# One more seven-product pair at the head of a feed-forward block: chunks 0 and 1 of the up-projection, and block sums of x from float copies

## The chip, the cores and the metric

The kernel runs on one core of a Trainium2 chip. A time is the device time of one execution in microseconds (us). TensorE (PE in the profile) does the matrix products, VectorE (DVE) and ScalarE (ACT) the elementwise work, GpSimd (POOL) a few elementwise operations and DMA issues, SyncE (SP) most DMA issues. Each engine takes its instructions strictly in the order in which they were written; a wait on a semaphore holds everything behind it on that engine.

## The reference

Two decoder layers over a residual stream h of 512 tokens by 1024 features, in float32. Each layer has an attention part (dilated windows in the first, forgetting attention with shared keys and values in the second), and then the part that matters here, the same in both layers:

```
def conv_ffn(xn, w_up, cw, cb, w_down):
    a = xn @ w_up                                  # (512, 1024) @ (1024, 5632)
    ap = jnp.pad(a, ((0, 0), (CONV_W - 1, 0), (0, 0)))
    a = sum(ap[:, j:j + T] * cw[j] for j in range(CONV_W)) + cb
    gate, val = jnp.split(a, 2, axis=-1)
    return (jax.nn.gelu(gate, approximate=True) * val) @ w_down
...
    h = h + rms_norm(mix, g[1])
    f = conv_ffn(rms_norm(h, g[2]), w_up[l], conv_w[l], conv_b[l], w_down[l])
    h = h + rms_norm(f, g[3])
```

## The kernel before

**Numbers.** Every operand of a product is split into a high part (rounded to the format that TensorE takes, by ScalarE) and a low part (the rest, by VectorE), and each product is three matmuls: high times high, high times low, low times high (`mm3`). The low part of some weights is made in another way: ScalarE writes the high part and the negated weight, and a DMA issued by GpSimd adds the weight and the parts up (`high_added`, or `high(key, True)`).

**The hidden features** are 22 chunks of 128, each with a gate and a value half, so two output tiles of 128 features by 512 tokens a chunk, one PSUM bank each. A chunk computed directly is two products over the whole of x (`up`, 24 matmuls of 512 columns each, or `feat_mm` in two halves of 256 columns). After it come the convolution (`tap`: one ScalarE and two VectorE operations a tile), the GELU and the product of gate and value (`product`), which goes to a DRAM buffer by a GpSimd DMA.

**Pairs.** Chunks 4 to 19 are taken two at a time as a 2 by 2 block product with seven instead of eight multiplications (class `Pair`). The weight blocks are called A11, A21, A22, A12 and their sums S1 to S4; x is cut into four blocks (features by tokens), and XA and XB hold sums of those blocks. The seven products are p_1 to p_7, each 24 matmuls of 256 columns. Several of them share a PSUM bank, and between them ScalarE copies a finished half aside (`keep_1`, `keep_7`, `keep_2`; the tile csum), to be added in later by VectorE (`sum_1`, `sum_3`, `sum_4`). The loop over the pairs interleaves seven products of one pair with the weight preparation of the next and the taps of the one before.

**The boundary ahead of it.** The attention's output projection ends in four blocks of 128 tokens. For each block, ScalarE and VectorE normalise it and add it into h, then normalise h (a square with a sum, a square root and a reciprocal, then `xn`), TensorE transposes it (eight transposes into the tiles xt_ps), ScalarE casts the high part and VectorE subtracts for the low part (`transpose_in`). Blocks 0 and 1 are through before the up-projection begins. Blocks 2 and 3 are transposed between the first products, which so far need only the first 256 tokens (LO): that is `first_products`, chunks 0 and 1, four tiles by LO, then four by HI.

**x block sums** (`sums_in`, tile xsum): GpSimd adds the high and low parts of x back together, VectorE makes the block differences, and ScalarE and VectorE split these into XA and XB. Chunks 2 and 3 run directly behind chunks 0 and 1, which covers this work; then the pairs begin.

**Order.** All of it is written out by hand (`manual_schedule`): the order of the program is the order on each engine. Weights are loaded by SP's queue through ten buffers (`W.load`), in the order of the list `pieces`, and prepared `W.ahead` pieces before they are used.

Of the kernel before, what the change touches and what calls it, by code (L numbers as in the profile page):

```python
# [9 lines left out]
F32 = mybir.dt.float32  # L10
# [14 lines left out]
BIG = 3.0e38  # L25


PAIRS = tuple(range(4, 20, 2))
ND = NF // 2
LAST = 3  # L30

# [84 lines left out]
def trunk_kernel(ctx, tc, x, norm_gains, w_qkv_a, w_o_a, w_q_b, w_o_b, kv_norm, w_kvf, b_f,  # L116
# [63 lines left out]
    dT = [tc.dram_tile([ND, 128, 2048], F32, name=f"dT{l}") for l in range(2)]  # L180

    def add_ffn(l):
        for c in range(NF):
            if c in PAIRS:
                for q, f in ((0, 0), (0, DFF), (1, DFF), (1, 0)):
                    add_block(w_up[l], q, f + c * 128)
            elif c - 1 not in PAIRS:
                add_cols(w_up[l], c * 128)
                add_cols(w_up[l], DFF + c * 128)
# [160 lines left out]
        lo = [t8([128, 4, T], F32R, name=f"{name}l{i}") for i in range(2)]  # L350
        return hi, lo

    def transpose_in(b, xn, xT, between=None):

        pts = []
        for i in range(2):
            pt = bank([128, 4, 128], name="xt_ps")
            for k in range(4):
                pe.transpose(pt[:, k, :], xn[:, (4 * i + k) * 128:(4 * i + k + 1) * 128], ident)
            pts.append(pt)  # L360
        s = slice(b * 128, b * 128 + 128)
        for i, pt in enumerate(pts):
            if i and between is not None:
                between()
            hi, lo = xT[0][i], xT[1][i]
            act.copy(hi[:, :, s], pt)
            dve.tensor_tensor(lo[:, :, s], pt, hi[:, :, s].bitcast(F32), ALU.subtract)

    def xs(xT, kc, s):
        return xT[0][kc // 4][:, kc % 4, s], xT[1][kc // 4][:, kc % 4, s]  # L370
# [60 lines left out]
    class Boundary:  # L431
# [26 lines left out]
        def transpose(self, b):  # L458
            if self.xT is None:
                self.xT = new_xT(self.name)  # L460
            transpose_in(b, self.xn.pop(b), self.xT)

    class SharedBoundary(Boundary):

# [76 lines left out]
                self.out(b)  # L541


    def first_products(bd, n):
        bd.norm(3)
        outs = [bank([128, T], name="first") for _ in range(n)]
        ws = []
        for i, o in enumerate(outs):
            ws.append(W.get())
            feat_mm(ws[i], bd.xT, o, LO)  # L550
            if i == 0:
                bd.transpose(2)
            if i == 2:
                bd.transpose(3)
        for w, o in zip(ws, outs):
            feat_mm(w, bd.xT, o, HI)
        return outs


    def load_conv(l):  # L560
        rows = t2([44, 4, 128], name="cv_rows")
        for j in range(3):
# [53 lines left out]
    def ffn(l, bd, cp, nxt, gain, ahead):  # L616
# [4 lines left out]
        def tap(bb, c, s, ps):  # L621
# [2 lines left out]
            dve.scalar_tensor_tensor(bb[:, s, 1:], ps[:, :T - 1], cp[:, 1, ch:ch + 1], bb[:, s, 1:], ALU.mult, ALU.add)  # L624
            dve.scalar_tensor_tensor(bb[:, s, 2:], ps[:, :T - 2], cp[:, 0, ch:ch + 1], bb[:, s, 2:], ALU.mult, ALU.add)

        class Chunk:

            def __init__(self, c, banks, room=None):
# [14 lines left out]

            def product(self):
                c = self.c
                if c - 1 in hc:
                    pool.dma_start(hD[c - 1], hc.pop(c - 1))
# [6 lines left out]

        def sums_in():

            v = [t8([128, 4, T], name=f"xsum{i}") for i in range(2)]
            for i in range(2):
                pool.tensor_tensor(v[i], xT[0][i].bitcast(F32), xT[1][i].bitcast(F32), ALU.add)  # L660
            yield
            dve.tensor_tensor(v[0][:, :, LO], v[0][:, :, HI], v[0][:, :, LO], ALU.subtract)
            dve.tensor_tensor(v[0][:, :, HI], v[1][:, :, HI], v[0][:, :, HI], ALU.subtract)
            yield
            dve.tensor_tensor(v[1][:, :, HI], v[1][:, :, HI], v[0][:, :, LO], ALU.subtract)
            dve.tensor_tensor(v[1][:, :, LO], v[1][:, :, LO], v[1][:, :, HI], ALU.subtract)
            yield
            for X, src in ((XA, v[0]), (XB, v[1])):
                X += [t8([128, 4, T], F32R, name="xsh"), t8([128, 4, T], F32R, name="xsl")]
                for k in (0, 2):  # L670
                    act.copy(X[0][:, k:k + 2], src[:, k:k + 2])
                    dve.tensor_tensor(X[1][:, k:k + 2], src[:, k:k + 2], X[0][:, k:k + 2].bitcast(F32), ALU.subtract)
                    yield

        def X(i):
            return xT[0][i], xT[1][i]
# [1 line left out]
        class Pair:  # L678
# [33 lines left out]
                dve.tensor_tensor(w[:, 1], self.f[key], w[:, 0].bitcast(F32), ALU.subtract)  # L712

            def prod(self, key, outs, x, s, start=False):
                w = self.t.pop(key).rearrange("p s (k c) -> p s k c", k=4)
                for i, o in enumerate(outs):
                    half_mm(o, w[:, :, :, i * 128:i * 128 + 128], x, s, start)

            def new_banks(self):
                return [bank([128, T], name="up") for _ in range(2)]  # L720
# [237 lines left out]

        def half_mm(o, w, x, s, start):
            for k in range(4):  # L960
                mm3(o, w[:, 0, k, :], w[:, 1, k, :], x[0][:, k, s], x[1][:, k, s], start and k == 0, k == 3, True)

        def up(w, o, kcs):
            wh, wl = (t.rearrange("p (k c) -> p k c", k=8) for t in w)
# [4 lines left out]
        base = W.n_get  # L969
        first = first_products(bd, 4)  # L970
        xT = bd.xT
        extra = sums_in()
        next(extra)
        done, last = Chunk(0, first[0:2]), Chunk(1, first[2:4])
        done.taps()
        next(extra)
        done.product()
        last.taps()
        W.ahead, W.ahead_dma = 1, 3
        W.split(base + 7)  # L980
        W.high_added()
        pairs = [Pair(c) for c in PAIRS]
        p, n = pairs[0:2]

        banks = p.new_banks()
        up(W.get(), banks[0], range(KD))
        for _ in range(3):
            next(extra, None)
        p.take("A11", "A21", "A22")
        p.high("A11", True)  # L990
        p.s1()
        p.s3()
        up(W.get(), banks[1], range(KD))
        run(extra)
        p.high("S1", True)
        done, last = last, Chunk(2, banks)

        banks = p.new_banks()
        up(W.get(), banks[0], range(KD))
        done.product()  # L1000
        last.tap(0)
        p.high("S3")
        p.s2()
        last.tap(1)
        p.high("S2")
        last.gelu()
        p.take("A12")
        p.low("S3")
        p.s4()
        up(W.get(), banks[1], range(KD))  # L1010
        p.high("A22", True)
        p.low("S2")
        last.product()
        n.take("A11")
        n.high("A11", True)
        p.p_1()
        p.keep_1()
        prev, m = None, [Chunk(3, banks)]

        for i, p in enumerate(pairs):  # L1020
            W.n_get += 4
            n, n2 = (pairs[i + k] if i + k < len(pairs) else None for k in (1, 2))
            a, b = m[0], m[-1]
            p.p_7()
            if prev:
                prev.sum_1()
            a.tap(0)
            p.high("A12", True)
# [12 lines left out]
            if prev:  # L1041
                b.tap(0)
            a.product()
            p.low("S4")
            p.p_5()
            p.sum_3()
            if n:
                n.s3()
            if prev:
                b.tap(1)  # L1050
            if n:
                n.high("A22", True)
# [12 lines left out]
            p.p_2()  # L1065
# [58 lines left out]
        pair_sums(3)  # L1124
        pair_lows(2)
        last.product()
        pool.dma_start(hD[NF - 1], hc.pop(NF - 1))

        down(nxt, ahead)
        W.ahead = 4  # L1130
# [776 lines left out]
```

## Time and profile before

| | |
|---|---|
| time, median of three runs | 1104.31 us (1103.82 to 1104.97) |
| the profiled execution | 1104.32 us, its span 1102.5 us, mean granted TensorE clock 0.998 |
| TensorE matmul busy | 1093.6 us, 99% of the span |
| VectorE, ScalarE, GpSimd busy | 892.3, 735.1, 231.5 us |
| the head of the up-projection in layer 0, first matmul to the first product p_7 | 178.0 to 227.4 us |
| the same head in layer 1 | begins at 759.8 us |

Rows of the profile have the start and the duration in us, the engine, the line in the kernel, the operation, output and input tiles, their sizes, and in brackets how long the engine had been idle and what released it. A duration runs to the end of the write; the next instruction on the same engine starts a little before that, so prices of queues are taken from one start to the next.

### The profile page before, as it was taken

To read this page: it belongs to the slowest core of one execution; us is meant where nothing else is said; L and a number is where in the kernel's file an instruction comes from. 1 tells how busy PE (TensorE), PEld (TensorE's weight loads), DVE (VectorE), ACT (ScalarE), POOL (GpSimd) and SP (SyncE) were. 2 spreads that over 40 slices of the span, in tenths; PEclk is the share of its full clock that TensorE was granted. 3 is DMA by queue.
4 is the path that set the end of the run, shared out by engine and by line. 5 is a ranking of instruction groups with operands and counts; after the bars stand their busy time and mean duration, and the time that the engine had idled before them with its cause. 6 is when DMAs were issued, how large, how long until landed. Compare 5 with 4: busy or idle time off the path is not lost.

```text
span 1102.5 us, 18986 instructions
## 1 busy us (share of the span) xinstructions
PE 1093.6 (99%) x6905; PEld 968.5 (88%) x6905; DVE 892.3 (81%) x1453; ACT 735.1 (67%) x1232; POOL 231.5 (21%) x335
## 2 busy tenths in 40 slices
PE   9999999999999999999999999999999999999997
PEld 6988889899999988888878888889999999988886
DVE  5897788967887789997698677868967887789994
ACT  6754575777788766576562588856677787856572
POOL 2632001322122211000000545600412122211000
PEclk9999999999999999999999999999999999999999
DMA  9699855499999999793447666783499999998872
GB/s 325 184 356 410 317 174 151 91 227 231 224 224 248 230 295 325 277 338 101 134 153 268 210 159 169 216 265 117 98 224 231 231 221 247 224 296 313 317 249 76
DMA packets 156006, 252.06 MB, mean 229 GB/s; under 512 B 12352, under 2 KB 99384, under 8 KB 155912
## 3 DMA queue, kind: packets, MB, share of 16 engines
q1 hardware_dynamic: 137576, 186.61, 51.1%
q0 software_dynamic: 18336, 64.24, 26.3%
q8 instruction: 54, 0.88, 0.3%
q14 instruction: 40, 0.33, 0.1%
HBM read 166.08 MB, written 39.63 MB: 187 GB/s over the span
## 4 chain that ended last, share of the span: by engine, by line
PE 85%; issue 9%; DVE 2%; ACT 2%; DMA 1%; POOL 1%; DVEq 0%; SPq 0%; POOLq 0%; ACTq 0%
PE up L288 12%; PE up L289 12%; PE up L290 12%; PE acc L288 8%; PE acc L290 8%; PE acc L289 8%; PE qk_ps L289 2%; PE qk_ps L288 2%; PE qk_ps L290 2%; PE s_ps L1733 2%; PE o_ps L1781 2%; PE pT_ps L1766 1%; PE first L290 1%; PE first L288 1%; PE first L289 1%
## 5 line engine op out<-in xcount | busy, mean ns | idle before, releaser
L288 PE MATMUL up<-xsh,w 128*128 128x256 f32 x512 | 144.9, 283 | 0.0
L289 PE MATMUL up<-xsl,w 128*128 128x256 f32 x512 | 144.9, 283 | 0.0
L290 PE MATMUL up<-xsh,w 128*128 128x256 f32 x512 | 144.9, 283 | 0.0
L288 PE MATMUL acc<-w 128*128 128x512 f32 (+1 forms) x311 | 120.7, 388 | 0.3 <-DVE mix L337 0.3
L290 PE MATMUL acc<-w 128*128 128x512 f32 (+1 forms) x311 | 120.6, 388 | 0.1
L705 ACT CAST w<-wraw 128x1024 fp32r<-128x1024 f32 x80 | 82.6, 1048 | 37.7 <-DVE wraw L689 37.7
L624 DVE SCALAR_TENSOR_TENSOR bb<-up,conv,bb 128x511 f32<-128x511 f32 x80 | 59.8, 748 | 57.2 <-ACT bb L623 57.0
L289 PE MATMUL acc<-w 128*128 128x512 f32 (+1 forms) x267 | 103.2, 387 | 0.0
L288 PEld LDWEIGHTS up<-xsh,w 128*128 128x128 f32 x512 | 98.3, 192 | 0.0
L289 PEld LDWEIGHTS up<-xsl,w 128*128 128x128 f32 x512 | 98.3, 192 | 0.0
L290 PEld LDWEIGHTS up<-xsh,w 128*128 128x128 f32 x512 | 98.3, 192 | 0.0
L623 ACT ACTIVATE bb<-up,conv 128x512 f32<-128x512 f32 x80 | 60.2, 780 | 32.7 <-DVE up L775 24.3
L288 PE MATMUL up<-xbh,w 128*128 128x256 f32 (+1 forms) x256 | 80.0, 312 | 0.1
L288 PE MATMUL up<-xch,w 128*128 128x256 f32 (+1 forms) x256 | 80.0, 312 | 0.1
L289 PE MATMUL up<-xbl,w 128*128 128x256 f32 (+1 forms) x256 | 79.2, 310 | 0.0
L289 PE MATMUL up<-xcl,w 128*128 128x256 f32 (+1 forms) x256 | 79.2, 310 | 0.0
L290 PE MATMUL up<-xbh,w 128*128 128x256 f32 (+1 forms) x256 | 79.2, 309 | 0.0
L290 PE MATMUL up<-xch,w 128*128 128x256 f32 (+1 forms) x256 | 79.2, 309 | 0.0
L708 POOL DMA_DIRECT2D w<-wraw x48 | 40.4, 841 | 183.5 <-ACT w L707 96.5
L76 DVE TENSOR_TENSOR w<-wraw,w 128x1024 fp32r<-128x1024 f32 x48 | 65.0, 1376 | 11.9 <-ACT w L58 11.4
L58 ACT CAST w<-wraw 128x1024 fp32r<-128x1024 f32 x62 | 63.7, 1051 | 15.8 <-PE v_ps L289 6.9
L290 PEld LDWEIGHTS acc<-w 128*128 128x128 f32 x311 | 58.4, 188 | 12.9 <-DVE w L817 0.9
(308 smaller groups left out, 3279.6 us busy)
## 6 DMA issues: line engine op xcount, KB each, us to landing
wraw<-in_w_up_dram SPq DMA_DIRECT2D x88, 512.0 KB, 6.6
w<-wraw POOLq DMA_DIRECT2D x62, 512.0 KB, 7.6
dT<-dsums SPq DMA_DIRECT2D x28, 512.0 KB, 7.5
dsums<-in_w_down_dram SPq DMA_DIRECT2D x22, 512.0 KB, 7.5
dsums<-in_w_down_dram SPq DMA_DIRECT2D x44, 256.0 KB, 6.6
hD<-hc POOLq DMA_DIRECT2D x44, 256.0 KB, 7.3
wraw<-dT SPq DMA_DIRECT2D x22, 512.0 KB, 6.8
dact<-hD SPq DMA_DIRECT2D x44, 256.0 KB, 5.3
```

Source lines behind the costliest of these rows:

```text
L58: self.nc.scalar.copy(pair[:, 0], raw)
L76: self.nc.vector.tensor_tensor(pair[:, 1], raw, pair[:, 0].bitcast(F32), ALU.subtract)
L288: pe.matmul(o, ah, bh, start=first, stop=False, skip_group_check=shared)
L289: pe.matmul(o, ah, bl, start=False, stop=False, skip_group_check=shared)
L290: pe.matmul(o, al, bh, start=False, stop=last, skip_group_check=shared)
L623: act.activation(bb[:, s, :], ps, AF.Identity, bias=cp[:, 3, ch:ch + 1], scale=cp[:, 2, ch:ch + 1])
L624: dve.scalar_tensor_tensor(bb[:, s, 1:], ps[:, :T - 1], cp[:, 1, ch:ch + 1], bb[:, s, 1:], ALU.mult, ALU.add)
L705: act.copy(w[:, 0], self.f[key])
L708: pool.dma_start(w[:, 1], self.f[key], accum_op=ALU.add)
L1733: pe.matmul(s[hh][:, :nn], qT[j][:, m, hh, i * 128:(i + 1) * 128], k, start=m == 0, stop=m == 1)
L1766: pe.transpose(o[:, k0 + k, :], p[:, hh, k * 128:(k + 1) * 128], ident)
L1781: pe.matmul(o[64 * hh:64 * hh + 64, i * 128:(i + 1) * 128], Vt[hd // 8][:, k, (hd % 8) * 64:(hd % 8) * 64 + 64], pT[j, i, hh][:, k, :], st ...
```

## The change

Chunks 0 and 1 are no longer computed directly but become one more pair, the first in the list `PAIRS`. The head is written anew: the product p_1 of this pair, the transposes of block 2, chunk 2's gate half by LO, the product p_2, the transposes of block 3, chunk 2's value half by LO, then both by HI, then chunk 3 directly, then the loop over the pairs, which for the first pair leaves out p_2 and A12. Since p_1 and p_2 of that pair use A11 and A12 before their sums are formed, these two blocks are loaded and split on their own and A11 and A12 loaded a second time for the sums. GpSimd's two additions go. In their place, ScalarE copies each transposed block once more, unrounded, into the tile xsum (two copies a block), and VectorE's block differences are made in two parts, 128 tokens at a time. The eight copies stand in `transpose_in`, behind the casts.

```
-PAIRS = tuple(range(4, 20, 2))
+PAIRS = 0, *range(4, 20, 2)
...
-    def transpose_in(b, xn, xT, between=None):
+    def transpose_in(b, xn, xT, keep):
...
             act.copy(hi[:, :, s], pt)
             dve.tensor_tensor(lo[:, :, s], pt, hi[:, :, s].bitcast(F32), ALU.subtract)
+        for i, pt in enumerate(pts):
+            act.copy(keep[i][:, :, s], pt)
...
-            v = [t8([128, 4, T], name=f"xsum{i}") for i in range(2)]
+            v = bd.x32
             for i in range(2):
-                pool.tensor_tensor(v[i], xT[0][i].bitcast(F32), xT[1][i].bitcast(F32), ALU.add)
-            yield
...
+                lo, hi = (slice(o + i * 128, o + i * 128 + 128) for o in (0, 256))
+                dve.tensor_tensor(v[0][:, :, lo], v[0][:, :, hi], v[0][:, :, lo], ALU.subtract)
+                dve.tensor_tensor(v[0][:, :, hi], v[1][:, :, hi], v[0][:, :, hi], ALU.subtract)
+                dve.tensor_tensor(v[1][:, :, hi], v[1][:, :, hi], v[0][:, :, lo], ALU.subtract)
+                dve.tensor_tensor(v[1][:, :, lo], v[1][:, :, lo], v[1][:, :, hi], ALU.subtract)
+                yield
...
+        W.ahead, W.ahead_dma = 1, 3
+        bd.norm(3)
+        p.t["A11"], w0, p.t["A12"], w1 = (W.get() for _ in range(4))
+        banks = [bank([128, T], name="first") for _ in range(2)]
+        p.p_1()
+        W.high_added()
+        bd.transpose(2)
+        feat_mm(w0, xT, banks[0], LO)
+        sums = sums_in()
+        next(sums)
+        p.keep_1()
+        W.high_added()
+        p.p_2()
+        bd.transpose(3)
+        feat_mm(w1, xT, banks[1], LO)
+        next(sums)
+        feat_mm(w0, xT, banks[0], HI)
+        feat_mm(w1, xT, banks[1], HI)
+        W.ahead_dma = 1
+        p.take("A11", "A21", "A22")
+        p.s1()
+        p.s3()
+        p.s2()
+        next(sums)
+        done, banks = Chunk(2, banks), p.new_banks()
+        done.tap(0)
+        p.high("S3")
+        p.high("S2")
+        p.take("A12")
+        p.s4()
+        up(W.get(), banks[0], range(KD))
+        next(sums)
+        done.tap(1)
+        done.gelu()
+        p.high("S1", True)
+        p.low("S3")
+        p.low("S2")
+        up(W.get(), banks[1], range(KD))
+        p.high("A22", True)
+        done.product()
+        n.take("A11")
+        n.high("A11", True)
```

ScalarE's order at block 3's norm (the square of h) and block 2's transposes, layer 0, in the kernel before. The number of partitions and elements follows the tiles; in brackets stands whose semaphore the row waits for.

```order
L295 ACTIVATE junk,s_1978<-h 128x1024 [waits DVE_49]
L297 ACTIVATE sd<-s_1978,eps_t 128x1 [waits Activation_49]
L366 CAST xbh_1858<-xt_ps 128x4x128 [waits PE_49]
L366 CAST xbh_1859<-xt_ps 128x4x128 [waits PE_49]
L58 CAST w<-wraw 128x1024 [waits DMAHW6_49]
L58 CAST w<-wraw 128x1024 [waits DMAHW7_49]
```

The same place in the changed kernel, up to the next weight:

```order
L299 ACTIVATE junk,s_1984<-h 128x1024 [waits DVE_49]
L301 ACTIVATE sd<-s_1984,eps_t 128x1 [waits Activation_49]
L58 CAST w<-wraw 128x1024 [waits DMAHW6_49]
L69 ACTIVATE w<-wraw 128x1024
L368 CAST xbh_1858<-xt_ps 128x4x128 [waits PE_49]
L368 CAST xbh_1859<-xt_ps 128x4x128 [waits PE_49]
L371 COPY xsum_1862<-xt_ps 128x4x128 [waits DVE_49]
L371 COPY xsum_1863<-xt_ps 128x4x128 [waits DVE_49]
L719 COPY csum<-up 128x256 x2
L58 CAST w<-wraw 128x1024 [waits DMAHW7_49]
```

A weight's cast and its negation now stand ahead of block 2's casts, the two float copies behind them, each waiting for VectorE, and then the two csum copies of `keep_1`.

TensorE's order in the changed kernel where chunk 2's gate half by LO ends (first) and p_2 begins (up, with the second feature half of x):

```order
L292 MATMUL first<-xbh_1859,w 128x256
L293 MATMUL first<-xbl_1861,w 128x256
L294 MATMUL first<-xbh_1859,w 128x256
L292 MATMUL up<-xbh_1859,w 128x256 [waits Activation_49]
L293 MATMUL up<-xbl_1861,w 128x256
L294 MATMUL up<-xbh_1859,w 128x256
```

Before, there stood at this place the third tile of `first_products` behind the second; now the first matmul of p_2 waits for ScalarE, into the bank from which `keep_1` copies.

More of the change, by code (lines that the diff above doesn't have):

```diff
@@ L182, in add_ffn @@
     def add_ffn(l):
[L183 to L189, printed above, removed]
+        for q in range(2):
+            add_block(w_up[l], q, 0)
+            add_cols(w_up[l], q * DFF + 2 * 128)
+        for q in range(2):
+            add_cols(w_up[l], q * DFF + 3 * 128)
+        for c in PAIRS:
+            for q, f in ((0, 0), (0, DFF), (1, DFF), (1, 0)):
+                add_block(w_up[l], q, f + c * 128)
+        for c in (NF - 2, NF - 1):
+            for q in range(2):
+                add_cols(w_up[l], q * DFF + c * 128)
         for j in range(ND):
@@ L362, in transpose_in @@
         for i, pt in enumerate(pts):
-            if i and between is not None:
-                between()
             hi, lo = xT[0][i], xT[1][i]
@@ L460, in transpose @@
                 self.xT = new_xT(self.name)
-            transpose_in(b, self.xn.pop(b), self.xT)
+                self.x32 = [t8([128, 4, T], name=f"xsum{i}") for i in range(2)]
+            transpose_in(b, self.xn.pop(b), self.xT, self.x32)
     class SharedBoundary(Boundary):
@@ L541, in part @@
                 self.out(b)
[L544 to L557, printed above, removed]
     def load_conv(l):
@@ L625, in tap, with send @@
             dve.scalar_tensor_tensor(bb[:, s, 2:], ps[:, :T - 2], cp[:, 0, ch:ch + 1], bb[:, s, 2:], ALU.mult, ALU.add)
+        def send():
+            for c in list(hc):
+                pool.dma_start(hD[c], hc.pop(c))
         class Chunk:
@@ L646, in product @@
                 c = self.c
-                if c - 1 in hc:
-                    pool.dma_start(hD[c - 1], hc.pop(c - 1))
+                send()
                 hc[c] = t2([128, T], name="hc")
@@ L672, in sums_in @@
                     dve.tensor_tensor(X[1][:, k:k + 2], src[:, k:k + 2], X[0][:, k:k + 2].bitcast(F32), ALU.subtract)
-                    yield
+                yield
         def X(i):
@@ L714, in prod @@
             def prod(self, key, outs, x, s, start=False):
-                w = self.t.pop(key).rearrange("p s (k c) -> p s k c", k=4)
+                w = self.t.pop(key)
+                w = [(w[i] if type(w) is tuple else w[:, i]).rearrange("p (k c) -> p k c", k=4) for i in range(2)]
                 for i, o in enumerate(outs):
-                    half_mm(o, w[:, :, :, i * 128:i * 128 + 128], x, s, start)
+                    half_mm(o, [t[:, :, i * 128:i * 128 + 128] for t in w], x, s, start)
             def new_banks(self):
@@ L960, in half_mm @@
             for k in range(4):
-                mm3(o, w[:, 0, k, :], w[:, 1, k, :], x[0][:, k, s], x[1][:, k, s], start and k == 0, k == 3, True)
+                mm3(o, w[0][:, k, :], w[1][:, k, :], x[0][:, k, s], x[1][:, k, s], start and k == 0, k == 3, True)
         def up(w, o, kcs):
@@ L967, in up @@
                 mm3(o, wh[:, kc, :], wl[:, kc, :], bh, bl, kc == 0, kc == KD - 1)
-        base = W.n_get
-        first = first_products(bd, 4)
         xT = bd.xT
[L972 to L981, printed above, removed]
         pairs = [Pair(c) for c in PAIRS]
         p, n = pairs[0:2]
-        banks = p.new_banks()
@@ L986, in ffn @@
-        up(W.get(), banks[0], range(KD))
-        for _ in range(3):
-            next(extra, None)
+        W.ahead, W.ahead_dma = 1, 3
[11 more added lines that the diff above has]
+        p.p_2()
@@ L989, in ffn @@
+        bd.transpose(3)
[4 more added lines that the diff above has]
+        W.ahead_dma = 1
         p.take("A11", "A21", "A22")
-        p.high("A11", True)
         p.s1()
         p.s3()
-        up(W.get(), banks[1], range(KD))
-        run(extra)
-        p.high("S1", True)
[L996 to L1007, printed above, removed]
+        p.s2()
[10 more added lines that the diff above has]
+        done.gelu()
+        p.high("S1", True)
         p.low("S3")
-        p.s4()
+        p.low("S2")
@@ L1010, in ffn @@
         up(W.get(), banks[1], range(KD))
         p.high("A22", True)
-        p.low("S2")
-        last.product()
+        done.product()
         n.take("A11")
         n.high("A11", True)
-        p.p_1()
-        p.keep_1()
+        W.ahead_dma = 3
         prev, m = None, [Chunk(3, banks)]
@@ L1027, in ffn @@
             a.tap(0)
-            p.high("A12", True)
+            if prev:
+                p.high("A12", True)
             p.keep_7()
@@ L1064, in ffn @@
                 n.high("S1", True)
-            p.p_2()
+            if prev:
+                p.p_2()
             if n:
@@ L1126, in ffn @@
         last.product()
-        pool.dma_start(hD[NF - 1], hc.pop(NF - 1))
+        send()
         down(nxt, ahead)
```

6 lines of the change are left out of this document (removed).

## The prediction

> **What bounds the kernel now.** I read the page's first part, then TensorE's waits, then its order of time at the head of a feed-forward block. In the fence, by line: busy time; who was waited for, total, times, longest; then start, duration, instruction.
>
> ```profile
> PE 1093.6 (99%) x6905; PEld 968.5 (88%) x6905; DVE 892.3 (81%) x1453; ACT 735.1 (67%) x1232; POOL 231.5 (21%) x335
> ...
> PE warm L248 <- DVE zero L243: 1.2, 1, 1.2
> ...
> 174.39 1.03 PE L359 MATMUL xt_ps<-ident,xn 128*128 128x128 f32 x8
> 178.01 0.28 PE L288 MATMUL first<-xbh,w 128*128 128x256 f32 x1
> 180.88 1.04 PE L359 MATMUL xt_ps<-ident,xn 128*128 128x128 f32 x8
> 187.50 1.03 PE L359 MATMUL xt_ps<-ident,xn 128*128 128x128 f32 x8
> 202.76 0.40 PE L288 MATMUL up<-xbh,w 128*128 128x512 f32 x1
> 224.55 0.28 PE L288 MATMUL up<-xbh,w 128*128 128x256 f32 x1
> 227.42 0.28 PE L288 MATMUL up<-xsh,w 128*128 128x256 f32 x1
> 247.58 0.28 PE L288 MATMUL up<-xsh,w 128*128 128x256 f32 x1
> ```
>
> TensorE bounds it: 1093.6 of 1102.5 us, and no wait over 1.2 us, none of them in this head. So each matmul removed counts in full, and so does each wait added. The prices come from starts. From 227.42 (first product of one pair) to 247.58 (the same of the next) lie seven products of 24 matmuls: 20.16 us for 168, 0.120 each at 256 columns. From 202.76 to 224.55 lie 96 matmuls of 512 columns: 0.227 each. Eight transposes take 0.87 (start 180.88, and the 48 matmuls to 187.50 take 5.76).
>
> **Matmuls removed.** Before, chunks 0 and 1 are 192 matmuls at 256 columns (23.04 us), chunks 2 and 3 are 96 at 512 (21.8), together 44.8 us. Now the pair is 168 at 256 (20.16), chunk 2 is 96 at 256 (11.52), chunk 3 is 48 at 512 (10.9), together 42.56. That is 2.24 us less in each layer, 4.5 in all. It stands only if the other engines keep up in the new head.
>
> **What is added to ScalarE's queue.** Each of the four x blocks gets two copies of its transposes to float, and by the order of rows each waits for VectorE, whose low-part subtraction reads the same bank. Behind them stand the squares of the next block's norm; ahead of the csum copies (keep_1, at 190 us below) stand block 2's casts and copies and a weight's cast and negation. The second product p_2 (line 292, "up", second half of x) waits on ScalarE: it writes the bank that keep_1 reads. So I walk ScalarE (ACT) and VectorE (DVE) from block 0 on with the rows of before:
>
> ```profile
> 168.84 1.07 ACT L366 CAST xbh<-xt_ps 128x512 fp32r<-128x512 f32 x2
> 169.78 1.08 ACT L295 ACTIVATE junk<-h 128x1024 bf16<-128x1024 f32 x1
> 176.12 1.08 ACT L295 ACTIVATE junk<-h 128x1024 bf16<-128x1024 f32 x1
> 181.29 1.06 ACT L295 ACTIVATE junk<-h 128x1024 bf16<-128x1024 f32 x1 [2.06 <-DVE h L344]
> 182.68 1.05 ACT L366 CAST xbh<-xt_ps 128x512 fp32r<-128x512 f32 x2
> 205.74 1.06 ACT L69 ACTIVATE w<-wraw 128x1024 fp32r<-128x1024 f32 x1
> L511 ACT COPY nT<-xt_ps 128x512 f32<-128x512 f32 x8 | 4.3, 583 | 0.0
> 226.18 0.37 ACT L728 COPY csum<-up 128x256 f32<-128x256 f32 x1 [2.59 <-PE up L290]
> ...
> 169.69 1.28 DVE L367 TENSOR_TENSOR xbl<-xt_ps,xbh 128x512 fp32r<-128x512 f32 x2
> 171.58 1.41 DVE L309 SCALAR_TENSOR_TENSOR xn<-h,rs,gain 128x512 f32<-128x512 f32 x2
> 172.91 0.68 DVE L337 TENSOR_TENSOR mix<-acc,gain 128x512 f32<-128x512 f32 x1
> 173.70 1.28 DVE L344 SCALAR_TENSOR_TENSOR h<-mix,rs,h 128x1024 f32<-128x1024 f32 x1
> 175.98 1.28 DVE L367 TENSOR_TENSOR xbl<-xt_ps,xbh 128x512 fp32r<-128x512 f32 x2
> 177.85 1.42 DVE L309 SCALAR_TENSOR_TENSOR xn<-h,rs,gain 128x512 f32<-128x512 f32 x2
> 179.97 1.28 DVE L344 SCALAR_TENSOR_TENSOR h<-mix,rs,h 128x1024 f32<-128x1024 f32 x1
> 188.76 1.29 DVE L367 TENSOR_TENSOR xbl<-xt_ps,xbh 128x512 fp32r<-128x512 f32 x2 [0.88 <-ACT xbh L366]
> ```
>
> The copies' price is L511's row, the same form: 0.58 us, the next instruction 0.47 after its start (1.07 for two casts).
>
> - Block 0: its low parts end at 169.69 + 1.28 = 170.97, so the second copy starts at 171.0 and the square of block 1 at 171.5, not 169.78 (+1.7). The normalised rows xn start 1.80 after the square (169.78 to 171.58): 173.3. TensorE transposes them at 174.4, still in time.
> - Block 1: after xn, VectorE needs 1.33 (171.58 to 172.91), 0.79 to the sum into h, 1.20 for that, 0.67 for the next mix: low parts from 177.3 to 178.55, not 177.26. p_1 needs the first half at 178.1: in time. Second copy 178.6, square of block 2 at 179.05, not 176.12 (+2.9). xn 1.73 later: 180.8, its halves done at 181.5 and 182.2. The transposes are due at 180.88 and now end at 182.7 instead of 181.75. **First wait: 0.9 us.**
> - Block 3's norm: h is summed at 180.8 + 2.12 = 182.9, done 184.2; its square starts there instead of 181.29, and frees ScalarE 1.39 later (181.29 to 182.68): 185.6. Then the weight's cast and negation, about 0.95 each: 187.5. Then block 2's casts, which before stood at 182.68. VectorE's low parts start 0.6 later and end 1.28 after that: 189.4. The second copy starts there, the first csum copy 0.47 later at 189.9, done 0.37 later: 190.3.
> - TensorE: transposes to 182.7, chunk 2's first half 2.88: p_2 is due at 185.55 and starts at 190.3. **Second wait: 4.75 us.**
>
> Bounds: with the two earlier copy pairs free, square 3 stays at 181.29 and the csum copy ends at 187.4 for a p_2 due at 184.63: 2.75 us in all. With 0.2 more at each of six handoffs: 6.9. I take the walk, 5.65, since every link has its row. Layer 1 repeats it.
>
> **Clock.** No stretch of before has such a gap inside, but both ends show TensorE's clock. In the window rows PEclk is the third number from the right:
>
> ```profile
> 1096.33 0.28 PE L290 MATMUL acc<-w 128*128 128x256 f32 x1
> 1098.00:1098.50 0.50, 0.00 (x0) 0.00 (x0) 0.50 (x2) 0.00 (x0) 0.00 (x0) 1.00 0.00 0
> 1098.70:1099.00 0.30, 0.00 (x0) 0.00 (x0) 0.30 (x1) 0.00 (x0) 0.00 (x0) 0.50 0.00 0
> 1.22 1.46 PE L248 MATMUL warm<-zero 128*128 128x512 bf16 x3 [1.22 <-DVE zero L243]
> 2.82 0.61 PE L248 MATMUL warm<-zero 128*128 128x512 bf16 x1
> 6.54 0.59 PE L248 MATMUL warm<-zero 128*128 128x512 bf16 x2
> ```
>
> The last matmul ended at 1096.6, and by 1098.7, 2 us later, the clock stood at one half. At the start, three matmuls of 0.61 end to end took 1.46 (0.42 apart); the last two are about 0.2 apart at 6.54: half speed for up to 5.3 us of work, 2.65 lost. So a gap of 4.75 us likely halves the clock, and p_2 and what follows lose 0 to 2.65 per layer. I take 2.0, nearer the upper end, as the fall needed only 2 us.
>
> The Trainium skill ("TensorE: Matmul & The Clock Gate", section "What's actually happening") has the clock fall after an idle window of about 3.4 us and rise after one as long of work. By it the loss would be 1.7 and the total 0.6 lower; a gap at my lower bound (2.75) would cost nothing, where the row of 2 us says it could. The row decides here.
>
> **What stays covered.** The rows that price it; the last two are DMA issues with their size and median time to landing:
>
> ```profile
> 189.53 10.19 POOL L660 TENSOR_TENSOR xsum<-xbh,xbl 128x2048 f32<-128x2048 f32 x2 [52.12 <-DVE xbl L367]
> 207.93 2.35 DVE L672 TENSOR_TENSOR xsl<-xsum,xsh 128x1024 fp32r<-128x1024 f32 x2
> 215.46 0.74 DVE L624 SCALAR_TENSOR_TENSOR bb<-up,conv,bb 128x511 f32<-128x511 f32 x1
> w<-wraw POOLq DMA_DIRECT2D x6, 512.0 KB, 5.6
> wraw<-in_w_up_dram SPq DMA_DIRECT2D x88, 512.0 KB, 6.6
> ```
>
> GpSimd's two additions go, which held only the block sums and nothing on TensorE. The new work behind block 3's transposes must end before the pair's S3 product, which TensorE reaches after 0.87 + 3 x 2.88 + 10.9 = 20.4 us. VectorE starts 1.26 after the transposes' start (187.50 to 188.76): low parts 1.3, four block subtractions 2.6 with 0.5 of waiting for copies, nine 1024-wide operations up to S3's low part at about 1.15 (10.4; L672: 2.35 for two), two taps at 1.45 each (twice 0.74): 17.7 in all, so done at 19.0 of 20.6 (S3's low part is read 0.24 after the first matmul). The margin of 1.6 us makes it free; beyond it each us counts. A22's low part comes by GpSimd's accumulating DMA (5.6 us to landing), about 24 after the transposes, and is read at 26.4. The second load of A11 and the reordered ones stand in SP's queue at least 10 us ahead of their readers, against 6.6 to landing.
>
> **Sum.** Per layer -2.24 + 0.9 + 4.75 + 2.0 = +5.4; twice, +10.8. The profiled execution took 1104.32 us (span 1102.5), the median of the runs shown is 1104.31, so the forecast is 1115.1.
>
> **Rivals.**
> - Forecast, stall with the clock halved: 1115.1, chance 0.58.
> - The same stall at full clock: 1104.3 + 2 x 3.4 = 1111.1. For it: the fall at the end came after a stretch already broken by short waits. Chance 0.20.
> - Faster, one mechanism: p_2 does not meet a late keep_1, because its wait is on an earlier ScalarE instruction or the float copies run beside the low parts, not behind them. Then 4.5 us are won: 1099.9. It decides below 2.24 us of waits per layer. For it: the matmul saving is sure, and no wait of such a kind is seen before. Against: the order of rows, and 2.75 remains even with free copies if the bank is the wait. Chance 0.11.
> - A further wait behind it: the 1.6 us margin at S3 or 2 us at A22 fails by 1 to 3 us a layer: 1117 to 1121. Chance 0.08.
> - Gain and waits cancel: 0.03.
>
> About 0.2% is what a measurement can tell from no change here. The cases give faster 0.11, same 0.03, slower 0.86. The range reaches from below the full-clock case with a shorter walk (1107) to the upper bound of the walk with the whole clock loss (2 x 7.3 = 14.6, 1118.9), and a little of the last rival: 1107 to 1120.
>
> **What would show it.** In the changed profile: TensorE's waits led by "up <- ACT csum" near 4 to 5 us, twice; a first wait "xt_ps <- DVE xn" near 0.9, twice; squares (line 299) of blocks 2 and 3 2.9 us later against the first matmul; PEclk 0.5 for some us behind p_2, matmuls 0.21 to 0.24 apart there; seven products in 20.16 us from then on with no wait. I am wrong if p_2 follows chunk 2's first half without a gap, if the float copies start before the low parts end, or if the gap leaves the clock whole.

## The result, and the profile after

| | before | after |
|---|---|---|
| time, median (five runs each, on the same chip) | 1104.18 us (1103.82 to 1104.97) | 1115.13 us (1114.83 to 1116.49) |
| ratio, 95% interval | | 1.0101 (1.0086 to 1.0116) |
| profiled execution, span | 1104.32, 1102.5 us | 1115.13, 1113.4 us |

The change makes the kernel 1.0% slower; 1115.1 was forecast. The page of after, its line of busy times, and TensorE's waits (who was waited for, total, times, longest):

```profile
PE 1093.6 (98%) x6953; PEld 970.3 (87%) x6953; DVE 900.0 (81%) x1481; ACT 759.5 (68%) x1272; POOL 216.0 (19%) x337
```
```profile
PE up L292 <- ACT csum L719: 9.1, 2, 4.6
PE warm L252 <- DVE zero L247: 1.2, 1, 1.2
PE xt_ps L363 <- DVE xn L313: 1.2, 2, 0.6
PE up L294 <- DMA w<-wraw: 0.7, 2, 0.4
```

TensorE's busy time is the same to the tenth though 4.5 us of work are gone from it: matmuls at half clock take longer, which is 2.8 us of it (1.49 and 1.33 in the two layers, below); the rest is not taken apart here. Three waits are new, each twice, once per layer: 4.6 for keep_1's copies, 0.6 for block 2's rows, 0.4 for a low part that a DMA adds up. Before, TensorE had no wait in this place.

The order of time in layer 0's head, ScalarE first, then TensorE:

```profile
170.25 1.19 ACT L371 COPY xsum<-xt_ps 128x512 f32<-128x512 f32 x2 [0.50 <-DVE xbl L369]
171.33 1.06 ACT L299 ACTIVATE junk<-h 128x1024 bf16<-128x1024 f32 x1
177.81 1.19 ACT L371 COPY xsum<-xt_ps 128x512 f32<-128x512 f32 x2 [1.73 <-DVE xbl L369]
178.89 1.06 ACT L299 ACTIVATE junk<-h 128x1024 bf16<-128x1024 f32 x1
184.05 1.06 ACT L299 ACTIVATE junk<-h 128x1024 bf16<-128x1024 f32 x1 [2.78 <-DVE h L348]
185.44 1.03 ACT L58 CAST w<-wraw 128x1024 fp32r<-128x1024 f32 x1
187.33 1.05 ACT L368 CAST xbh<-xt_ps 128x512 fp32r<-128x512 f32 x2
188.65 1.18 ACT L371 COPY xsum<-xt_ps 128x512 f32<-128x512 f32 x2 [0.28 <-DVE xbl L369]
189.73 0.65 ACT L719 COPY csum<-up 128x256 f32<-128x256 f32 x2
...
177.85 0.28 PE L292 MATMUL up<-xbh,w 128*128 128x256 f32 x1
181.50 1.23 PE L363 MATMUL xt_ps<-ident,xn 128*128 128x128 f32 x8 [0.62 <-DVE xn L313]
190.16 0.58 PE L292 MATMUL up<-xbh,w 128*128 128x256 f32 x1 [4.56 <-ACT csum L719]
194.53 1.03 PE L363 MATMUL xt_ps<-ident,xn 128*128 128x128 f32 x8
```

The float copies stand idle for 0.50 and 1.73 us until VectorE's low parts are through, and the squares behind them (line 299) start at 171.33, 178.89 and 184.05, where they stood at 169.78, 176.12 and 181.29. The csum copies start at 189.73, and p_2 at 190.16. It ends with the transposes of block 3 at 194.53: 4.37 us for 24 matmuls that take 2.88 elsewhere. The clock in the window rows (third number from the right) says why:

```profile
185.50:186.50 1.00, 0.10 (x1) 0.00 (x0) 0.90 (x3) 1.00 (x3) 0.00 (x0) 1.00 0.16 55
189.00:190.00 1.00, 0.00 (x0) 0.00 (x0) 0.91 (x2) 0.99 (x4) 0.00 (x0) 0.97 1.02 361
191.00:192.00 1.00, 1.00 (x6) 1.00 (x6) 0.97 (x2) 1.00 (x2) 0.00 (x0) 0.50 1.07 209
194.00:195.00 1.00, 1.00 (x11) 1.00 (x11) 0.00 (x0) 0.00 (x0) 0.00 (x0) 1.00 1.17 225
```

It is whole until about 190.0, 4.4 us after the last matmul ended at 185.6, and half until about 193.4.

### The profile page after: what moved, and what is told of

It is laid out like the page before. It is cut to its first block, busy times and chain, and to the rows that moved or that the text cites. A ratio compares the mean times of both kernels' runs of the same rounds, so it can differ in the third digit from the quotient of the medians.

```text
span 1113.4 us, 19165 instructions
## 1 busy us (share of the span) xinstructions
PE 1093.6 (98%) x6953; PEld 970.3 (87%) x6953; DVE 900.0 (81%) x1481; ACT 759.5 (68%) x1272; POOL 216.0 (19%) x337
## 4 chain that ended last, share of the span: by engine, by line
PE 82%; DVE 5%; ACT 4%; issue 4%; DMA 4%; POOL 0%; SPq 0%; DVEq 0%; POOLq 0%; ACTq 0%
PE up L292 10%; PE up L294 10%; PE up L293 10%; PE acc L294 7%; PE acc L292 7%; PE acc L293 7%; DMA w<-wraw 3%; PE v_ps L292 2%; PE v_ps L294 2%; PE v_ps L293 2%; PE qk_ps L293 2%; PE qk_ps L292 2%; PE qk_ps L294 2%; PE s_ps L1723 2%; PE o_ps L1771 1%
## 5 line engine op out<-in xcount | busy, mean ns | idle before, releaser
L294 PE MATMUL up<-xsh,w 128*128 128x256 f32 x576 | 163.2, 283 | 0.7 <-DMA w<-wraw 0.7
L293 PE MATMUL up<-xsl,w 128*128 128x256 f32 x576 | 163.0, 283 | 0.0
L292 PE MATMUL up<-xsh,w 128*128 128x256 f32 x576 | 163.0, 283 | 0.0
L695 ACT CAST w<-wraw 128x1024 fp32r<-128x1024 f32 x86 | 88.9, 1050 | 41.6 <-DVE wraw L679 41.6
L294 PEld LDWEIGHTS up<-xsh,w 128*128 128x128 f32 x576 | 110.6, 192 | 1.1 <-DMA w<-wraw 1.1
L292 PEld LDWEIGHTS up<-xsh,w 128*128 128x128 f32 x576 | 110.6, 192 | 0.1
L293 PEld LDWEIGHTS up<-xsl,w 128*128 128x128 f32 x576 | 110.6, 192 | 0.1
L613 DVE SCALAR_TENSOR_TENSOR bb<-up,conv,bb 128x511 f32<-128x511 f32 x84 | 62.8, 748 | 53.9 <-ACT bb L612 53.7
L292 PE MATMUL up<-xbh,w 128*128 128x256 f32 (+1 forms) x264 | 81.5, 309 | 4.6 <-ACT csum L719 4.6
L292 PE MATMUL up<-xch,w 128*128 128x256 f32 (+1 forms) x264 | 81.3, 308 | 4.6 <-ACT csum L719 4.6
L612 ACT ACTIVATE bb<-up,conv 128x512 f32<-128x512 f32 x84 | 63.0, 778 | 31.1 <-DVE up L766 22.7
L294 PE MATMUL up<-xch,w 128*128 128x256 f32 (+1 forms) x264 | 80.4, 304 | 0.1
L294 PE MATMUL up<-xbh,w 128*128 128x256 f32 (+1 forms) x264 | 80.3, 304 | 0.0
L58 ACT CAST w<-wraw 128x1024 fp32r<-128x1024 f32 x58 | 59.8, 1051 | 15.4 <-PE v_ps L293 6.9
L294 PEld LDWEIGHTS acc<-w 128*128 128x128 f32 x311 | 58.4, 188 | 12.8 <-DVE w L808 0.9
L292 PEld LDWEIGHTS acc<-w 128*128 128x128 f32 x311 | 58.4, 188 | 12.4 <-DVE mix L341 0.7
```

The source lines that it names most:

```text
L58: self.nc.scalar.copy(pair[:, 0], raw)
L292: pe.matmul(o, ah, bh, start=first, stop=False, skip_group_check=shared)
L293: pe.matmul(o, ah, bl, start=False, stop=False, skip_group_check=shared)
L294: pe.matmul(o, al, bh, start=False, stop=last, skip_group_check=shared)
L612: act.activation(bb[:, s, :], ps, AF.Identity, bias=cp[:, 3, ch:ch + 1], scale=cp[:, 2, ch:ch + 1])
L695: act.copy(w[:, 0], self.f[key])
```

## The experiments

Every run was timed beside the kernel before on the same chip, 1104.0 to 1104.2 us there.

**keep_1 earlier.** The csum copies are moved, nothing else:

```
-        bd.norm(3)
         p.t["A11"], w0, p.t["A12"], w1 = (W.get() for _ in range(4))
         ...
         p.p_1()
+        p.keep_1()
+        bd.norm(3)
         W.high_added()
         ...
         next(sums)
-        p.keep_1()
```

> The changed kernel with one thing moved: keep_1's two csum copies stand on ScalarE directly behind p_1, ahead of block 3's norm, instead of behind block 2's casts and float copies. Theory: p_2 waits for these copies and for nothing else. They then end near 181.5 us, four microseconds before p_2 is due at 185.6, so the wait of 4.56 and the 1.49 lost at half clock both go in each layer: 1115.1 - 2 x 6.05 = 1103.0 us, 'up <- ACT csum' gone from TensorE's waits, the wait of 0.62 at block 2's transposes unchanged. Rival: p_2 is held by something that merely ends at the same time (block 2's float copies, its half of x, the loaded A12): 1115, wait under another name. Second rival: the wait goes but VectorE and GpSimd are not ready for the pair's S3 or A22 any earlier: 1105 to 1110 with a new wait there.

Measured 1109.42 us (1107.21 to 1111.54), ratio 1.0044 (1.0032 to 1.0056). The wait for csum is gone and p_2 starts at 185.57 instead of 190.16, at full clock: the theory holds for the place. But only 5.7 us of the 12.1 came through, as the second rival had it. The six runs lie far apart, and the longer ones have the lower mean clock (0.999 for the two shortest, 0.996 for the longest); the traced one, 1109.71, lost the clock once. That the others differ in how often they lost it is likely, but not shown by a trace. The waits; then the DMA of S1's low part (size, us from issue to landing), issued at 208.23, the issue of A22's, its time to landing and TensorE's row; then the clock behind that:

```profile
PE up L294 <- DMA w<-wraw: 4.0, 2, 2.0
PE warm L252 <- DVE zero L247: 1.2, 1, 1.2
PE xt_ps L363 <- DVE xn L313: 1.1, 2, 0.6
```
```profile
w<-wsum POOLq DMA_DIRECT2D x1, 512.0 KB, 5.2
...
210.13 0.83 POOL L698 DMA_DIRECT2D w<-wraw  x1 [1.05 <-DVE w L702]
w<-wraw POOLq DMA_DIRECT2D x1, 512.0 KB, 7.9
...
218.11 0.39 PE L294 MATMUL up<-xsh,w 128*128 128x256 f32 x1 [2.03 <-DMA w<-wraw]
```
```profile
219.50:220.50 1.00, 1.00 (x7) 1.00 (x7) 0.43 (x1) 0.00 (x0) 0.32 (x1) 0.50 1.12 233
```

A22's accumulating DMA is issued at 210.13 and its product p_4 waits for it until 218.11: eight microseconds. S1's, issued 1.9 us ahead in the same queue, needed 5.2; A22's landed 4.7 us behind it. TensorE came to p_4 five microseconds earlier than in the changed kernel, the issue only three and a half (213.55 there), because S1's preparation stands ahead of it on ScalarE and GpSimd. The wait of 2.0 comes in both layers and in layer 0 it halves the clock once more.

**A22 ahead of S1**, on top of that:

```
-        p.high("S1", True)
+        p.high("A22", True)
         ...
         up(W.get(), banks[1], range(KD))
-        p.high("A22", True)
+        p.high("S1", True)
```

> The kernel with keep_1 early, and besides A22's high part, negation and accumulating DMA ahead of S1's, instead of behind them. Theory: the new wait of 2.03 at the pair's product of A22 (line 294, 'up <- DMA w<-wraw') comes only from A22 standing behind S1 on ScalarE and GpSimd. Its DMA was issued at 210.1 and landed at 218.1, two microseconds after the product wanted it; issued 1.9 earlier it lands as the product starts. The wait falls from 2.03 to 0.3 or less, the clock stays whole behind it, and S1's part, needed 2.9 us later, lands in time: 1115.1 - 2 x (4.56 + 1.49 + 0.38) + 2 x 0.8 (a wait for block 3's parts seen with keep_1 early) = 1103.8. Rival: the landing is late because the DMA engines are loaded at that time, not because of its place: 1107 to 1110, wait of 1.5 to 2 at A22 or now at S1.

Measured 1104.93 us (1104.21 to 1105.79), ratio 1.0003 (0.9994 to 1.0012): 1.1 above the number, 4.5 below the run before.

```profile
PE xt_ps L363 <- DVE xn L313: 1.1, 2, 0.6
PE up L294 <- DMA w<-wraw: 1.0, 1, 1.0
```
```profile
208.56 0.84 POOL L698 DMA_DIRECT2D w<-wraw  x1 [15.21 <-DVE bb L613]
w<-wraw POOLq DMA_DIRECT2D x1, 512.0 KB, 5.1
...
w<-wsum POOLq DMA_DIRECT2D x1, 512.0 KB, 7.8
```

Issued at 208.56, A22's part is in time, and there is no wait at p_4 in either layer. Its transfer now needs 5.1 us, and S1's, which is second here, 7.8: the place was the cause, not a load of the DMA engines at that time. Most of the missing 1.1 is a new wait of 1.0 in layer 0, at the first product of the next pair, whose A11 stands behind both in GpSimd's queue.

**The float copies behind the next norm**, blocks 0 and 1 (`transpose` returns them as a function, `half` calls it):

```
-                    self.transpose(self.order[i - 2])
+                copies = self.transpose(self.order[i - 2]) if i >= 2 else None
                 if i >= 1:
                     self.norm(self.order[i - 1])
+                if copies:
+                    copies()
```

> The changed kernel with the float copies of blocks 0 and 1 issued behind the next block's square and square root instead of ahead of them; blocks 2 and 3 unchanged. Theory: the copies ahead of the squares cause the first wait and part of the second. Squares of blocks 2 and 3 go back to about 176.1 and 181.3 us, the wait at block 2's transposes (0.62 in the changed kernel) to 0, and the csum copy ends near 187.4 for a p_2 due at 184.7: a wait of 2.75. If the clock falls only after 4.4 us as it did in the changed kernel, it stays whole: 1115.1 - 2 x (0.8 + 1.8 + 1.5) = 1106.9; if it falls after 2 us as at the program's end: 1109.9. Rival: the squares are late for another reason (VectorE's sums into h): waits unchanged, 1115.

Measured 1109.62 us (1107.69 to 1110.44), ratio 1.0044 (1.0032 to 1.0056).

```profile
PE up L292 <- ACT csum L723: 5.3, 2, 2.6
```
```profile
176.36 1.08 ACT L299 ACTIVATE junk<-h 128x1024 bf16<-128x1024 f32 x1
...
181.55 1.06 ACT L299 ACTIVATE junk<-h 128x1024 bf16<-128x1024 f32 x1 [1.82 <-DVE h L348]
...
187.23 0.66 ACT L723 COPY csum<-up 128x256 f32<-128x256 f32 x2
```

The squares are back, the first wait is gone, and what is left at csum is 2.6, where the prediction's lower bound for free early copies said 2.75. Of the two numbers for the clock, the second was right: this gap cost p_2 as much as the gap of 4.6 (table below). That is the traced run, 1109.74. Two of the five runs were 1.9 us shorter, with a mean clock of 0.998 against 0.996; one stretch of 3.4 us at half clock lowers the mean by 0.0015, so one layer probably kept its clock there, though no trace shows it.

**The gap filled.** 38 matmuls whose results are never read, ahead of p_2:

```
         W.high_added()
+        spare = bank([128, T], name="spare")
+        wf = p.t["A12"][0]
+        for i in range(38):
+            pe.matmul(spare[:, LO], wf[:, 0:128], wf[:, 0:256], start=i == 0, stop=i == 37)
         p.p_2()
```

> The changed kernel with 38 extra matmuls of 256 columns (a spare bank, results never read) between chunk 2's first half and p_2: 38 x 0.120 = 4.56 us of work in the place of the wait of 4.56. Theory: the wait vanishes from the list without making the kernel slower, since TensorE was standing there anyway, and the clock stays at 1.00, so p_2 takes 2.88 instead of 4.37: 1115.1 - 2 x 1.49 = 1112.1. Rival: the slow p_2 was not the clock but its operands (low parts, weights arriving piece by piece): 1115 and p_2 still near 4.4. Second rival: the extra matmuls take time of their own: 1118 to 1124.

Measured 1113.59 us (1113.30 to 1113.78), ratio 1.0085 (1.0072 to 1.0098). More work on the busiest engine, and 1.5 us less time.

```profile
190.11 0.39 PE L292 MATMUL up<-xbh,w 128*128 128x256 f32 x1
190.33 0.28 PE L293 MATMUL up<-xbl,w 128*128 128x256 f32 x1
190.45 0.28 PE L294 MATMUL up<-xbh,w 128*128 128x256 f32 x1
```
```profile
PE up L294 <- DMA w<-wraw: 2.3, 2, 2.1
```

p_2 starts where it started, with 0.12 from matmul to matmul, and takes 2.98: the clock was the cause. Layer 0 keeps the 1.4 us. Layer 1 gains 1.2 and loses 1.8 of its lead at A22's DMA (a wait of 2.1 there). That is the missing half.

**How long a gap must be.** The same with 13, 21 and 30 matmuls, two or three runs each:

> The changed kernel with 13 extra matmuls of 256 columns ahead of p_2 (1.56 us; a spare bank, never read), so that of the wait of 4.56 about 3.0 us are left. The point of the three runs is how long TensorE must stand for its clock to halve: gaps of 4.6, 2.8 and 2.6 us cost p_2 1.5 us in both layers, gaps of 1.9 to 2.1 cost 1.5 in some places and nothing in others. Theory: it is a threshold near 2 us, and the loss behind it does not grow with the gap: here p_2 takes 4.4 instead of 2.88 in both layers, and the time is that of the changed kernel, 1114 to 1115. Rival: the loss grows with the gap: p_2 about 3.9.

> As the run before, with 21 extra matmuls (2.5 us), 2.0 us left. Theory of the threshold: p_2 takes either 2.9 or 4.4, in one layer, both or none: 1112 to 1115. Rival of the graded loss: about 3.5 in both.

> As the two runs before, with 30 extra matmuls (3.6 us), about 1.0 us left. Theory of the threshold: the clock stays whole, p_2 takes 2.9 in both layers, 1112 to 1114 as with the gap filled. Rival of the graded loss: about 3.2 in both.

Measured 1114.41, 1113.56 and 1112.04 us. From the starts in the traces, all runs together (the wait by the profile, and the time of p_2, layer 0 and layer 1):

| kernel | wait before p_2 | p_2 takes |
|---|---|---|
| changed | 4.6 | 4.37, 4.22 |
| 13 matmuls | 3.0 | 4.29, 4.37 |
| float copies late | 2.6 | 4.47, 4.46 |
| 21 matmuls | 2.0 | 4.46, 2.98 |
| 30 matmuls | 1.0 | 2.97, 2.97 |
| 38 matmuls | none | 2.98, 2.98 |

The loss is 1.3 to 1.6 us or nothing, and does not grow with the gap. For these runs the edge is near 2 us, and there one layer loses and the other does not. The traces say why. In each of them the changes of the clock lie whole multiples of 3.413 us apart (in the changed kernel 189.95, 193.36, 777.04 and 780.45), so the clock goes by windows of that length. With 21 matmuls, these are the windows that hold the start of the gap, each with the window behind it (TensorE's busy time, then the clock, third from the right):

```profile
186.58:189.99 3.41, 1.40 (x12) 1.00 0.50 145
189.99:193.40 3.41, 3.38 (x16) 0.50 0.81 162
773.67:777.08 3.41, 1.64 (x14) 1.00 0.41 124
777.08:780.50 3.42, 3.15 (x26) 1.00 0.87 183
```

In layer 0 almost the whole gap lies in one window, which is left with 2.01 us without a matmul, and the next window is at half clock. In layer 1 the end of the gap lies in the next window, 1.77 us are left, and the clock stays whole. Over the twelve traces, every window at whole clock that was idle for 1.87 us or more was followed by half clock (eleven inside the programs, from 1.94 up, the others at their ends), and none that was idle for 1.77 or less. By these numbers, as an estimate, a single gap under 1.8 us costs nothing, one over 3.7 (twice 1.87, so that one window gets enough of it) always does, and in between it depends on how the gap falls into the windows.

**Block sums from GpSimd, a block at a time**, in the changed kernel:

```
         for i, pt in enumerate(pts):
-            act.copy(keep[i][:, :, s], pt)
+            hi, lo = xT[0][i], xT[1][i]
+            pool.tensor_tensor(keep[i][:, :, s], hi[:, :, s].bitcast(F32), lo[:, :, s].bitcast(F32), ALU.add)
```

> The changed kernel without float copies on ScalarE: GpSimd adds high and low part of each x block instead, two additions per block behind its low parts. Theory: the eight copies leave ScalarE's queue, the first wait (0.62) goes, squares stand as before the change, and the csum copies come directly behind block 2's casts, near 186.5 for a p_2 due at 184.7: a wait of about 1.8 and no clock drop. 1115.1 - 2 x (0.8 + 2.8 + 1.5) = 1104.9, plus up to 2 us a layer if block 3's sums, about 2.6 us on GpSimd by its 10.19 for the whole, come late for the pair's S3: 1105 to 1109. Rival: the copies cost nothing and the order of keep_1 alone makes the stall: 1113 to 1115.

Measured 1115.26 us (1112.85 to 1116.30), ratio 1.0097 (1.0084 to 1.0110): no better than the changed kernel, a miss of 6 to 10 us. The first wait is gone, but:

```profile
PE up L292 <- ACT csum L720: 5.6, 2, 2.8
PE up L294 <- DMA w<-wraw: 4.0, 3, 1.9
```
```profile
177.44 2.99 POOL L372 TENSOR_TENSOR xsum<-xbh,xbl 128x512 f32<-128x512 f32 x2 [3.88 <-DVE xbl L369]
...
178.06 2.92 DVE L313 SCALAR_TENSOR_TENSOR xn<-h,rs,gain 128x512 f32<-128x512 f32 x2
...
184.71 1.42 DVE L313 SCALAR_TENSOR_TENSOR xn<-h,rs,gain 128x512 f32<-128x512 f32 x2
```

While GpSimd adds, VectorE's pair of multiplications for xn takes 2.92 us; without it, 1.42. So the sum into h and the next square are late again (183.00 against 181.55 with the copies late), and the csum wait stays at 2.8 and keeps its clock loss (in layer 1 p_2 even takes 5.29, at half clock for two windows). The Trainium skill ("SBUF — State Buffer", section "Who interferes with whom") states that a VectorE instruction with two inputs in SBUF contends with a GpSimd instruction that reads SBUF; these rows agree. A22's wait of 1.9 with another half-clock stretch takes the rest. That ScalarE's copies cost nothing, the rival, is not shown by this: one delay took the place of another.

**The copies alone**, in the kernel before, without the pair: `transpose_in` as in the change, and `sums_in` with

```
-            v = [t8([128, 4, T], name=f"xsum{i}") for i in range(2)]
-            for i in range(2):
-                pool.tensor_tensor(v[i], xT[0][i].bitcast(F32), xT[1][i].bitcast(F32), ALU.add)
+            v = bd.x32
```

> The kernel before, with the block sums made from ScalarE's float copies as in the change, and without the pair. Theory: the copies cost only the first wait (xt_ps <- xn, 0.6 to 0.9 a layer), since no csum copy stands behind block 2's in that order; GpSimd's 10.19 us that go held nothing on TensorE: 1104.2 + 2 x 0.6 to 0.9 = 1105.4 to 1106.0, no clock drop. Rival: the copies alone make most of the loss (block 3's norm late for its transposes): 1108 to 1113. Second rival: the earlier block sums gain something: 1103 or less.

Measured 1107.66 us (1107.23 to 1108.44), ratio 1.0031 (1.0019 to 1.0042), between theory and rival.

```profile
PE xt_ps L359 <- DVE xn L309: 1.1, 2, 0.6
PE first L289 <- DVE xbl L365: 0.6, 1, 0.6
PE first L289 <- DVE xcl L365: 0.6, 1, 0.6
```

By the starts the first wait delays TensorE by 1.0 a layer, near the 0.9 that was forecast for the change. The second, 0.85, was left out of the expectation: block 2's copies push back two weight casts and with them VectorE's low parts of these weights (190.00 to 192.28), and block 3's low parts, which stand behind those, come late for the products by HI.

**All at once.** keep_1 behind p_1, the copies late, the second weight behind block 3's casts, and in the head:

```
         done.tap(0)
+        p.high("A22", True)
         p.high("S3")
         p.high("S2")
+        p.low("S3")
         p.take("A12")
-        p.s4()
         ...
         done.tap(1)
-        done.gelu()
         p.high("S1", True)
-        p.low("S3")
         p.low("S2")
+        p.s4()
+        done.gelu()
         up(W.get(), banks[1], range(KD))
-        p.high("A22", True)
```

> The changed kernel with every wait seen so far attended to: keep_1 behind p_1; float copies of each block behind the next norm; the second weight's cast and negation behind block 3's casts; A22's parts ahead of S3's and S1's; S3's low part ahead of S4's sum and of the second split; GELU behind S1. No arithmetic is changed. Theory: the change's saving of 2.24 per layer was real and only these waits hid it: no TensorE wait over 0.4 in either head, 1104.2 - 2 x 2.24 = 1099.7, with up to 0.5 a layer for small waits: 1099.7 to 1100.7. Rival: with one wait gone another engine (VectorE before the pair's S3 product, ScalarE, the weight loads) takes its place: 1102 or more.

Measured 1099.78 us (1099.38 to 1100.35), ratio 0.9958 (0.9946 to 0.9971): faster than both kernels, by 4.4 us against before, where 2 x 2.24 = 4.5 was the saving in matmuls.

```profile
PE warm L252 <- DVE zero L247: 1.2, 1, 1.2
PE qk_ps L292 <- ACT w L62: 0.4, 1, 0.4
```

These are TensorE's longest waits now, and neither is in a head.

## Why the prediction was right

Since the last run has the changed kernel's matmuls without its waits, the difference of the two traces, matmul by matmul, gives each term by itself. TensorE's lead of that run over the changed kernel grows in four places of each layer; it is read where the matmuls are evenly spaced again.

| step of the prediction | forecast per layer | by the starts, layer 0 | layer 1 |
|---|---|---|---|
| matmuls removed | -2.24 | -2.2 (1099.78 against 1104.17: -4.4 for two) | -2.2 |
| first wait, block 2's rows | 0.9 | 0.97 | 0.90 |
| second wait, p_2 for keep_1's copies | 4.75 | 4.72 | 4.73 |
| p_2 at half clock | 2.0 | 1.49 | 1.33 |
| S3 and A22, covered | 0 | 0.65, all at A22 | 0.53, all at A22 |
| sum | 5.4 | 5.6 | 5.3 |

- **The walk along ScalarE's queue** held at each link: the squares 1.55, 2.8 and 2.8 us later (forecast 1.7, 2.9, 2.9; against the first matmul, which came 0.16 earlier, just that), the csum copies from 189.73 (189.9), p_2 at 190.16 (190.3). That the wait was for keep_1 and nothing beside it, the run with keep_1 earlier showed. The lower bound of 2.75 came out as 2.6 once the early copies were out of the way.
- **The clock term was mis-sized**: 2.0 was taken from the bounds 0 to 2.65, and 1.33 to 1.49 measured. The upper bound was read from the program's start, where half speed lasted up to 5.3 us; here it lasted 3.41, in which 16 matmuls start 0.213 apart instead of 0.120. The prediction's other estimate, 1.7 by the Trainium skill ("TensorE: Matmul & The Clock Gate", section "What's actually happening"), which has the clock rise after about 3.4 us of work, was nearer. On when the clock falls the order is reversed: a gap of 2.75 would cost nothing by an idle window of 3.4 us, and in the traces windows that were idle for 1.9 to 2.8 us of their 3.41 were enough. There the row of the program's end (2 us) was right.
- **A22 was not covered.** The step reckoned 5.6 us from issue to landing, and a margin of 2 us. The issue came about when it was reckoned, 19.0 us after block 3's transposes, and 5.6 us is near the time of a transfer that goes alone or first (S1's 5.2). But A22's stands 1.9 us behind S1's in one queue: issued at 213.55, it was read at 221.47, nearly eight later, and p_4 had been due at 221.1. The margin was gone even behind a stall of six microseconds that had held TensorE back. The page's median over all the accumulating DMAs of this kind, 8.7 (7.6 before), mixes both cases. S3 held to within 0.3 us in all runs.
- The two mis-sized terms, the clock 0.5 and 0.7 too much in the two layers and A22 0.65 and 0.53 too little, cancelled. The agreement with 1115.1 to a tenth is luck in that; the two waits, 5.65 of the 7.65 us of loss, were right by their links. (The terms of the step on the matmuls removed add up to 42.58 and not 42.56, which changes nothing here.)
- **The rivals.** The stall at full clock (1111.1) falls with the clock rows and the filled gap. The faster case fails because the wait was on the late copies, and the case in which gain and waits cancel with it. The further wait behind the stall (chance 0.08) was there in small.

## What to carry to other kernels

A copy that only saves another engine's work is dear if it is put into a queue ahead of something on the critical path: walk the queue link by link with the durations of the rows, and look for who waits on the last instruction of it. A wait that is removed gives back less than its length while the next resource keeps its old place in the order (here 5.7 of 12.1 us); move its preparation with it. For the time of a DMA look at what stands ahead of it in its queue: the time of one that goes first (5.2 us) was 2.7 short for the second of two.

## What the runs showed of the hardware that was not expected

- TensorE's clock went by windows of 3.41 us. It halved behind a window in which TensorE was idle for 1.87 us or more, and not behind 1.77 or less, so gaps of 2.0 us halved it in some places only. In p_2 the loss is then 1.3 to 1.6 us whatever the gap (2.4 once, in layer 1 of the run with GpSimd's sums, where the first half-clock window was again idle for 0.74 us and a second followed). Since it comes as a step, 38 useless matmuls in a gap of 4.6 us made the kernel 1.5 us faster.
- Since the fall comes with the end of a window, it can come after the gap: with keep_1 earlier, TensorE went on at 218.11 at full clock and was at half from about 219.1, 3 us after the gap began.
- Accumulating DMAs of 512 KB that are issued 1.9 us apart land one behind the other: in the two heads of nine runs the first needed 5.1 to 5.3 us and the second 7.7 to 7.9 (9.6 once), whichever of the two weights came first.
- GpSimd's additions beside VectorE doubled the time of VectorE's multiplications with two SBUF inputs (2.92 against 1.42 us), so moving work from ScalarE to GpSimd moved the delay to VectorE.
